# FFN activations turned in 32x32 blocks on VectorE and placed through DRAM, in a two-layer decoder trunk on one core

## The chip, the cores and the metric

The kernel runs on one core of a Trainium2 chip. The metric is the device time of one execution in microseconds. The core's engines are named as the profile names them: PE is TensorE (matmuls; PEld its weight load), DVE is VectorE, ACT is ScalarE, POOL is GpSimd, and SP is SyncE, whose queue issues the transfers.

## The reference

The reference computes a trunk of two layers on 256 tokens of width 1024, in float32. Each layer is

```python
x = x + 0.5 * swiglu(rms_norm(x, ffn1_norm[layer]), w_gate, w_up, w_down)
x = x + mixer(rms_norm(x, mix_norm[layer]), rms_norm(mem, mem_norm[layer]))
x = x + 0.5 * swiglu(rms_norm(x, ffn2_norm[layer]), w_gate, w_up, w_down)

def swiglu(h, w_gate, w_up, w_down):
    return (jax.nn.silu(h @ w_gate) * (h @ w_up)) @ w_down
```

with an inner FFN width of 2816. The mixer of layer 0 is a chunkwise mLSTM beside a cross-attention to 256 memory tokens; the mixer of layer 1 is a dilated sliding-window attention, with shared keys and values computed from layer 0's output, beside the same kind of cross-attention. The four FFNs are where the change lies.

## The kernel before

**Tiles.** The tokens lie in two tiles of 128 (`t` = 0 and 1). Each FFN's inner width is cut into `NB` = 11 blocks of `FB` = 256 columns. For block `b` and token tile `t`, `gu(b, t)` makes the gate and up products together: a PSUM bank (gups) of 128 tokens by 512 columns, 256 of gate and 256 of up, over eight chunks of the model width. `dn(b, t)` adds the down products of that block to two accumulators (acc) of 512 columns that stay in PSUM for the whole FFN.

**Precision.** Every float32 product is made from three matmuls. Each operand is split into `hi`, its value rounded to fp32r, and `lo`, the remainder (`split`, line 558: a copy on ScalarE, a subtraction on VectorE); `mm3` (line 551) multiplies hi by lo, hi by hi and lo by hi. So gu(b, t) has 24 matmuls and dn(b, t) has 12.

**Between the two products.** `hidden(b, t)` (line 761) makes the activation h: silu on ScalarE, then a multiplication on VectorE, 128 tokens by 256 columns. The down product needs h with its columns on the partitions, so TensorE transposes two squares of 128x128 into a PSUM tile (tph), and `split` copies them from there into hh and hl, the stationary operands of the down product.

**Weights.** All weights stand in one DRAM array in the order of use, as written by `_stream` (line 44) and `_pack` (line 108). A unit is 128 x 1024 values, 512 KB: a gate/up block takes four, a down block two. `load_unit` transfers a unit into one of `RAW` = 6 raw tiles on SyncE's queue, `emit_unit` casts and subtracts it into one of `RING` = 8 ring slots (hi and lo). A ring slot is free again when both token tiles have used it.

**Order.** Nothing is scheduled by a compiler: the instructions are written in the order in which the program calls them, and each engine runs its own in that order. TensorE's order is given by the loops of `ffn` (line 757). What else has to be done is held in chains of steps (`spawn`, `step`), and a planner (`_Model`, line 152 on) with its own estimates of costs decides after each group of matmuls which chain's next step is written next. Its times decide the order only; waits between engines are by semaphores. `wait` lets a chain wait for others, `finish` writes a chain to its end, `freed_bank` writes until a bank is read. The order of the products in an FFN before the change is gu(0), gu(1), dn(0), gu(2), dn(1), and so on to gu(8), dn(7), gu(9); then gu(10, 0), dn(8, 0), gu(10, 1), dn(9, 0), dn(10, 0), and dn(8, 1) to dn(10, 1). The first two blocks of the first FFN are special: `opening` (line 706) and `both` (line 741) run them for both token tiles at once, into accumulator banks, while the first transfers arrive. Two blocks, `MEMORY`, have the memory tokens' key and value product behind them.

**A path through DRAM** exists already: `shared_kv` writes a small tile (diag) to DRAM and reads it back in another layout (bias).

Of the kernel before, what the change touches and what calls it, by code (L numbers as in the profile page):

```python
# [8 lines left out]
F32 = mybir.dt.float32  # L9
F32R = mybir.dt.float32r  # L10
BF16 = mybir.dt.bfloat16
AF = mybir.ActivationFunctionType
ALU = mybir.AluOpType
# [4 lines left out]
P = 128  # L18
# [15 lines left out]
LATER = 1.5  # L34
EARLY = 0.0
WARM = 9
MEMORY = {(0, 1, 4): 0, (1, 1, 4): 1}
TAIL = 3

# [4 lines left out]
def _stream():  # L44

    units = []

    def proj(key, name, index, cols, each):
        k = 0
        while k < NK:  # L50
            n = min(each, NK - k)
            width = n * sum(b - a for _, a, b in cols)
            units.append((key + (k,), (name, index, cols, k, n), width))
            k += n

    def rows(key, name, index, order):
        for c in order:
            units.append((key + (c,), (name, index, None, c, 1), D))

    def single(key, name, index, lo, hi, kper):  # L60
        proj(key, None, index, ((name, lo, hi),), kper)

    def memory(layer):
        for m in range(2):
            units.append((("memT", layer, m), ("memT", None, None, m, 1), D))
        single(("mkv", layer), "w_mem_kv", layer, 0, 512, 2)

    def ffn(layer, which):
        g, u, d = (f"ffn{which}_w_{s}" for s in ("gate", "up", "down"))

        def gu(b):
            lo, hi = b * FB, (b + 1) * FB
            proj(("gu", layer, which, b), None, layer, ((g, lo, hi), (u, lo, hi)), 2)

        def dn(b):
            for c in range(2):
                units.append((("dn", layer, which, b, c), (d, layer, None, 2 * b + c, 1), D))

        gu(0)
        for b in range(1, NB - 1):  # L80
            gu(b)
            if (layer, which, b) in MEMORY:
                memory(MEMORY[layer, which, b])
            if b < NB - 2:
                dn(b - 1)
        gu(NB - 1)
        for b in range(NB - 3, NB):
            dn(b)

    ffn(0, 1)  # L90
    single(("a", "gq"), "a_gq", None, 0, 264, 3)
    for key, lo in (("q0", 0), ("k0", MW), ("v0", 2 * MW),
                    ("q1", 384), ("k1", MW + 384), ("v1", 2 * MW + 384),
                    ("o0", 3 * MW), ("o1", 3 * MW + 384)):
        single(("a", key), "a_w_in", 0, lo, lo + 384, 2)
    rows(("ao",), "a_w_out", 0, A_ORDER)
    ffn(0, 2)
    for b in range(3):
        single(("kv", b), "w_kv", None, b * 512, (b + 1) * 512, 2)
    ffn(1, 1)  # L100
    for b in range(2):
        single(("bq", b), "b_w_q", 0, b * 512, (b + 1) * 512, 2)
    rows(("bo",), "b_w_out", 0, B_ORDER)
    ffn(1, 2)
    return units


def _pack(units, w):

    parts = []  # L110
    for _, src, _ in units:
        name, index, cols, k, n = src
        if cols is None:
            a = w[name][index] if index is not None else w[name]
            parts.append(a[k * P:(k + 1) * P, :].reshape(-1))
            continue
        pieces = []
        for cname, lo, hi in cols:
            a = w[cname][index] if index is not None else w[cname]
            pieces.append(a[k * P:(k + n) * P, lo:hi].reshape(n, P, hi - lo))  # L120
        parts.append(np.concatenate(pieces, axis=2).transpose(1, 0, 2).reshape(-1))
    return np.concatenate(parts)
# [135 lines left out]
class _Engine:  # L258
# [5 lines left out]
    def __getattr__(self, method):  # L264
        call, model, name = getattr(self.engine, method), self.model, self.name

        def traced(out, *args, **kw):
            call(out, *args, **kw)  # L268
            aps = [a for a in list(args) + list(kw.values()) if isinstance(a, bass.AP)]
            outs = [out] + [kw[k] for k in ("accum_out",) if k in kw]  # L270
            ins = [a for a in aps if a is not kw.get("accum_out")]
            n = out.free_size()
            if name == "sync":
                model.run(name, max(n * out.partition_size() * 4 / 360e3, 0.06), outs, ins, 2.0)
                return
            fixed, each = model.COST[name]
            cost = fixed + each * n
            if method == "tensor_reduce":
                cost = fixed + each * ins[0].free_size()
            if name == "vector" and any(a.free_size() == 1 for a in ins):  # L280
                cost += 0.06
            if method == "reciprocal":
                cost = fixed + 8 * each * n
            if kw.get("accum_out") is not None or isinstance(kw.get("scale"), bass.AP):
                cost += 0.09
            if name == "gpsimd" and ALU.pow in args:
                cost = 0.4 + 0.07 * n
            for a in args if method == "activation" else ():
                table = model.TABLES.get(a) if isinstance(a, AF) else None
                if table is not None and table != model.table:  # L290
                    model.table = table
                    cost += 1.3
            model.run(name, cost, outs, ins)
        return traced
# [30 lines left out]
class _Kernel:  # L325
# [429 lines left out]


    def ffn(self, layer, which, after, memory=None):
        nc = self.nc
        acc, chains, hT = [], {}, {}

        def hidden(b, t):
            def steps(ps):
                yield from self.wait(self.stats[t])
                rstd = self.rstd[t]
                sil = self.work.tile([P, FB], F32, tag="ta", bufs=4, name="sil")
                nc.scalar.activation(sil, ps[:, :FB], AF.Silu, scale=rstd)
                yield
                h = self.work.tile([P, FB], F32, tag="ta", bufs=4, name="h")
                nc.vector.scalar_tensor_tensor(h, ps[:, FB:], rstd, sil, ALU.mult, ALU.mult)
                yield FREE  # L770
                tp = yield from self.psum("tp", [P, 512], "tph")
                for c in range(2):
                    self.transpose(tp[:, c * P:(c + 1) * P], h[:, c * P:(c + 1) * P], self.ident)
                yield
                hh = self.work.tile([P, FB], F32R, tag="hh", bufs=5, name="hh")
                hl = self.work.tile([P, FB], F32R, tag="hl", bufs=5, name="hl")
                yield from self.split(hh, hl, tp[:, :FB])
                self.leave("tp")
                hT[b, t] = (hh, hl)
            return steps  # L780

        def gu(b, t):
            chains[b, t] = self.block(t, ("gu", layer, which, b), 512, 2, hidden(b, t))

        def dn(b, t):
            if len(acc) == t:
                if t == 0:
                    self.finish(chains[0, 0], chains[0, 1])
                else:
                    self.freed_bank(*[chains[1, i] for i in range(2)])  # L790
                acc.append([self.acc.tile([P, 512], F32, tag="acc", name=f"acc{t}{h}")
                            for h in range(2)])
            self.finish(chains.pop((b, t)))
            hh, hl = hT.pop((b, t))
            last = b == NB - 1
            pairs = [(c, h) for h in range(2) for c in range(2)] if last else \
                    [(c, h) for c in range(2) for h in range(2)]
            for n, (c, h) in enumerate(pairs):
                wh, wl = self.get("dn", layer, which, b, c)
                self.until(max(self.model.ready(a) for a in (wl, hl)))  # L800
                s = slice(c * P, (c + 1) * P)
                f = slice(h * 512, (h + 1) * 512)
                self.mm3(acc[t][h], (hh[:, s], hl[:, s]), (wh[:, f], wl[:, f]),
                         b == 0 and c == 0, last and c == 1)
                if last and n % 2:
                    nc.vector.scalar_tensor_tensor(self.x[t][:, f], acc[t][h], 0.5, self.x[t][:, f],
# [6 lines left out]
        for b in range(NB - 1):  # L813
            if (layer, which, b) == (0, 1, 0):
                ps = [self.acc.tile([P, 512], F32, tag="acc", name="gups") for _ in range(2)]
                self.opening(ps, ("gu", 0, 1, 0))
                for t in range(2):
                    chains[0, t] = self.spawn(hidden(0, t)(ps[t]))
                continue
            if (layer, which, b) == (0, 1, 1):  # L820
                ps = [self.acc.tile([P, 512], F32, tag="acc", name="gups") for _ in range(2)]
                self.both(ps, ("gu", 0, 1, 1))
                for t in range(2):
                    chains[1, t] = self.spawn(hidden(1, t)(ps[t]))
            else:
                for t in range(2):
                    gu(b, t)
            if (layer, which, b) in MEMORY:
                memory()
            if 0 < b < NB - 2:  # L830
                for t in range(2):
                    dn(b - 1, t)
        gu(NB - 1, 0)
        dn(NB - 3, 0)
        gu(NB - 1, 1)
# [692 lines left out]
```

## Time and profile before

| | us |
|---|---|
| three runs | 1021.74, 1021.84, 1021.99 |
| median | 1021.84 |
| the profiled execution | 1021.66 |
| its span, first to last instruction | 1019.9 |
| TensorE busy | 1011.5 |
| TensorE weight loads | 833.3 |
| VectorE busy | 616.8 |
| ScalarE busy | 551.0 |
| GpSimd busy | 56.5 |

The profile is of one execution. Lines such as L268 and L541 are helpers: nearly every instruction has the line of the helper that writes it, so groups are read by their tiles: gups and acc are the FFN's products, tph the transposed activation, raw, hi and lo the weights. Matmuls overlap their neighbours, so a matmul's own duration is longer than the distance between two starts. Idle time of an engine that doesn't set the end costs nothing.

### The profile page before, as it was taken

How to read it: one execution, taken by the hardware profiler on the slowest of the kernel's cores; microseconds unless marked ns; L12 is line 12 of the kernel's file. 1: busy time of each engine (PE TensorE's matmuls, PEld its weight loads, DVE VectorE, ACT ScalarE, POOL GpSimd, SP SyncE). 2: the span in 40 equal slices, each digit the busy share in tenths (PEclk: the TensorE clock that was granted, in tenths of full speed). 3: DMA queues.
4: the chain of work that ended last, by engine and by line, in shares of the span. 5: the costliest groups of instructions: out<-in, count | busy, mean ns of one | idle time of the engine just before them, and what ended most of it. 6: DMA issues, size and time to landing. Idle time of an engine off the chain costs nothing.

```text
span 1019.9 us, 13096 instructions
## 1 busy us (share of the span) xinstructions
PE 1011.5 (99%) x4849; PEld 833.3 (82%) x4849; DVE 616.8 (60%) x884; ACT 551.0 (54%) x883; POOL 56.5 (6%) x82
## 2 busy tenths in 40 slices
PE   9999999999999999999999999999999999999998
PEld 6887888898988888888878888888887788888886
DVE  5855655566976746454586654745467875545452
ACT  7645545478675645454466543645457674545441
POOL 0021000010010000000021020100012000000000
PEclk9999999999999999999999999999999999999999
DMA  9854764345455565656466555656452345656531
GB/s 353 297 184 164 272 210 166 109 155 167 139 161 191 183 208 170 202 178 194 165 206 229 174 165 200 243 170 204 144 189 63 104 168 204 199 172 202 170 124 42
DMA packets 54329, 184.63 MB, mean 181 GB/s; under 512 B 6332, under 2 KB 8052, under 8 KB 54264
## 3 DMA queue, kind: packets, MB, share of 16 engines
q1 hardware_dynamic: 54120, 183.75, 53.9%
q8 instruction: 38, 0.62, 0.3%
q14 instruction: 27, 0.22, 0.1%
q10 hardware_dynamic: 144, 0.04, 0.0%
HBM read 182.70 MB, written 1.07 MB: 180 GB/s over the span
## 4 chain that ended last, share of the span: by engine, by line
PE 87%; DVE 2%; ACT 1%; issue 1%; POOL 0%; DVEq 0%; ACTq 0%
PE gups L541 42%; PE acc L541 21%; PE aps L541 7%; PE oacc L541 4%; PE kvps L541 3%; PE bqps L541 2%; PE tph L548 2%; PE tps L548 1%; PE mkvps L541 1%; PE sc L541 1%; DVE s L268 1%; DVE lo L268 1%; PE ms L541 1%; PE po L541 1%; PE pn L541 0%
## 5 line engine op out<-in xcount | busy, mean ns | idle before, releaser
L268 DVE TENSOR_TENSOR lo<-raw,hi 128x1024 fp32r<-128x1024 f32 (+3 forms) x351 | 411.8, 1192 | 151.8 <-ACT hi L268 139.0
L268 ACT CAST hi<-raw 128x1024 fp32r<-128x1024 f32 (+3 forms) x351 | 352.9, 1020 | 103.9 <-PE acc L541 58.7
L541 PE MATMUL gups<-lo,xh 128*128 128x512 f32 x704 | 278.4, 397 | 0.2 <-DVE lo L268 0.2
L541 PE MATMUL gups<-hi,xh 128*128 128x512 f32 x704 | 273.6, 390 | 0.4 <-ACT hi L268 0.4
L541 PE MATMUL gups<-hi,xl 128*128 128x512 f32 x704 | 273.7, 391 | 0.0
L541 PEld LDWEIGHTS gups<-hi,xl 128*128 128x128 f32 x704 | 132.1, 188 | 28.5
L541 PEld LDWEIGHTS gups<-hi,xh 128*128 128x128 f32 x704 | 132.5, 188 | 27.7 <-ACT hi L268 1.7
L541 PEld LDWEIGHTS gups<-lo,xh 128*128 128x128 f32 x704 | 132.2, 188 | 26.9 <-DVE lo L268 0.8
L541 PE MATMUL acc<-lo,hh 128*128 128x512 f32 x352 | 140.9, 400 | 0.0
L541 PE MATMUL acc<-hi,hl 128*128 128x512 f32 x352 | 137.6, 391 | 0.0
L541 PE MATMUL acc<-hi,hh 128*128 128x512 f32 x352 | 137.2, 390 | 0.0
L268 ACT ACTIVATE sil<-gups,rstd 128x256 f32<-128x256 f32 x88 | 41.7, 475 | 172.0 <-PE gups L541 171.9
L268 DVE SCALAR_TENSOR_TENSOR h<-gups,rstd,sil 128x256 f32<-128x256 f32 x88 | 42.2, 481 | 130.0 <-ACT sil L268 130.0
L541 PEld LDWEIGHTS acc<-hi,hl 128*128 128x128 f32 x352 | 66.0, 188 | 14.1
L541 PEld LDWEIGHTS acc<-hi,hh 128*128 128x128 f32 x352 | 66.3, 188 | 12.5
L541 PEld LDWEIGHTS acc<-lo,hh 128*128 128x128 f32 x352 | 66.1, 188 | 12.3
L268 ACT CAST hh<-tph 128x256 fp32r<-128x256 f32 x88 | 32.6, 372 | 79.1 <-PE tph L548 79.1
L268 DVE TENSOR_TENSOR hl<-tph,hh 128x256 fp32r<-128x256 f32 x88 | 37.2, 424 | 39.7 <-ACT hh L268 39.6
L541 PE MATMUL aps<-lo,xh 128*128 128x384 f32 (+1 forms) x144 | 49.5, 344 | 0.0
L541 PE MATMUL aps<-hi,xl 128*128 128x384 f32 (+1 forms) x144 | 47.5, 330 | 0.0
L541 PE MATMUL aps<-hi,xh 128*128 128x384 f32 (+1 forms) x144 | 47.4, 329 | 0.0
L268 ACT ACTIVATE xh<-tps,gains 128x128 fp32r<-128x128 f32 x96 | 27.2, 372 | 21.2 <-PE tps L548 21.2
(179 smaller groups left out, 918.6 us busy)
## 6 DMA issues: line engine op xcount, KB each, us to landing
raw<-in_wts SPq DMA_DIRECT2D x311, 512.0 KB, 4.6
raw<-in_wts SPq DMA_DIRECT2D x32, 384.0 KB, 3.5
bias<-diag SPq DMA_DIRECT2D x1, 1536.0 KB
xraw<-in_xT SPq DMA_DIRECT2D x4, 256.0 KB, 5.9
x<-in_x SPq DMA_DIRECT2D x2, 512.0 KB, 9.0
mt<-in_mem SPq DMA_DIRECT2D x2, 512.0 KB
out<-x SPq DMA_DIRECT2D x4, 256.0 KB, 2.0
raw<-in_wts SPq DMA_DIRECT2D x2, 396.0 KB, 3.5
```

The costliest lines, as they stand in the source:

```text
L268: call(out, *args, **kw)
L541: self.pe.matmul(out, lhsT=lhsT, rhs=rhs, start=start, stop=stop)
L548: self.pe.transpose(out, in_, ident)
```

## The change

A function `turned` names the blocks that are handled anew: all but the last of each FFN, and in the first FFN not blocks 0 and 1. That makes 38 of 44. For these, the activation isn't transposed on TensorE. VectorE turns each 32x32 square of h within itself (`nc.vector.transpose`), for both token tiles into one tile hb of 128 x 512. A new chain `placed` then writes hb to DRAM (256 KB) and reads it back so that the squares come to lie on the right partitions (ht, runs of 128 values, 512 bytes), both on SyncE's queue, and splits ht in one cast and one subtraction of 128 x 512 for both token tiles. The activation's columns end in another order within their 256 than before; `_pack` puts the rows of the down weights into the same order. The tiles hb, ht, hh and hl come from a pool of their own in each FFN.

The order of the products becomes gu(0), gu(1), gu(2), dn(0), gu(3), dn(1), and so on to gu(9), dn(7), and then ends as before. The stream of weights follows that order.

The planner gets a price for transfers on queues other than SyncE's; the program has one such transfer, at its start.

```diff
+def turned(layer, which, b):
+    return b < NB - 1 and ((layer, which) != (0, 1) or b > 1)
...
             if (layer, which, b) in MEMORY:
                 memory(MEMORY[layer, which, b])
-            if b < NB - 2:
-                dn(b - 1)
+            if b > 1:
+                dn(b - 2)
...
+            a = a[k * P:(k + 1) * P, :]
+            if cols:
+                a = a.reshape(4, 32, -1).transpose(1, 0, 2)
+            parts.append(a.reshape(-1))
...
+            if method == "dma_start" and name != "sync":
+                model.run(name, 1.0 if name == "gpsimd" else 0.1, outs, ins, 2.5)
+                return
...
+        def hidden_blocks(b, t):
+            def steps(ps):
+                h = self.work.tile([P, FB], F32, tag="ta", bufs=4, name="h")
+                yield from activated(ps, t, h)
+                if b not in blocks:
+                    blocks[b] = fp.tile([P, 4, 2, 2, 32], F32, tag="hb", bufs=1, name="hb")
+                nc.vector.transpose(blocks[b][:, :, :, t, :].rearrange("p j c t -> p c j t"),
+                                    h.rearrange("p (c j e) -> p c j e", c=2, j=4))
+            return steps
+
+        def placed(b, before):
+            yield from self.wait(*before)
+            hb = blocks.pop(b)
+            d = self.dram.tile([P, 512], F32, tag="hd", bufs=4, name="hd")
+            nc.sync.dma_start(d, hb.rearrange("p j c t e -> p (j c t e)"))
+            yield
+            ht = fp.tile([P, 4, P], F32, tag="ht", bufs=1, name="ht")
+            nc.sync.dma_start(ht, bass.AP(d.tensor, d.offset, [[P, P], [32 * 512, 4], [1, P]]))
+            yield
+            hh = fp.tile([P, 4, 4, 32], F32R, tag="hh", bufs=4, name="hhb")
+            hl = fp.tile([P, 4, 4, 32], F32R, tag="hl", bufs=4, name="hlb")
+            yield from self.split(*(a.rearrange("p c i e -> p i c e") for a in (hh, hl)),
+                                  ht.rearrange("p i (c e) -> p i c e", c=4))
+            for t in range(2):
+                hT[b, t] = [tuple(a[:, 2 * c + t].rearrange("p i e -> p (i e)") for a in (hh, hl))
+                            for c in range(2)]
+
+        def follow(b, t, chain):
+            made[b, t] = chains[b, t] = chain
+            if turned(layer, which, b) and t == 1:
+                chains[b, 0] = chains[b, 1] = self.spawn(placed(b, [made[b, 0], made[b, 1]]))
...
         def dn(b, t):
             if len(acc) == t:
-                if t == 0:
-                    self.finish(chains[0, 0], chains[0, 1])
-                else:
-                    self.freed_bank(*[chains[1, i] for i in range(2)])
+                self.freed_bank(*[made[t, i] for i in range(2)])
...
-            if 0 < b < NB - 2:
+            if 1 < b < NB - 1:
                 for t in range(2):
-                    dn(b - 1, t)
+                    dn(b - 2, t)
```

More of the change, by code (lines that the diff above doesn't have):

```diff
@@ L76, in dn @@
             for c in range(2):
-                units.append((("dn", layer, which, b, c), (d, layer, None, 2 * b + c, 1), D))
+                rows = "turned" if turned(layer, which, b) else None
+                units.append((("dn", layer, which, b, c), (d, layer, rows, 2 * b + c, 1), D))
         gu(0)
@@ L112, in _pack @@
         name, index, cols, k, n = src
-        if cols is None:
+        if cols is None or cols == "turned":
             a = w[name][index] if index is not None else w[name]
-            parts.append(a[k * P:(k + 1) * P, :].reshape(-1))
+            a = a[k * P:(k + 1) * P, :]
+            if cols:
+                a = a.reshape(4, 32, -1).transpose(1, 0, 2)
+            parts.append(a.reshape(-1))
             continue
@@ L757, in ffn, with ffn_in, activated @@
     def ffn(self, layer, which, after, memory=None):
+        with ExitStack() as ctx:
+            self.ffn_in(layer, which, after, memory, self.pool(ctx, f"ffn{layer}{which}"))
+    def ffn_in(self, layer, which, after, memory, fp):
         nc = self.nc
-        acc, chains, hT = [], {}, {}
+        acc, chains, hT, blocks, made = [], {}, {}, {}, {}
+        def activated(ps, t, out):
+            yield from self.wait(self.stats[t])
+            rstd = self.rstd[t]
+            sil = self.work.tile([P, FB], F32, tag="ta", bufs=4, name="sil")
+            nc.scalar.activation(sil, ps[:, :FB], AF.Silu, scale=rstd)
+            yield
+            nc.vector.scalar_tensor_tensor(out, ps[:, FB:], rstd, sil, ALU.mult, ALU.mult)
+            yield FREE
         def hidden(b, t):
             def steps(ps):
[L763 to L767, printed above, removed]
                 h = self.work.tile([P, FB], F32, tag="ta", bufs=4, name="h")
-                nc.vector.scalar_tensor_tensor(h, ps[:, FB:], rstd, sil, ALU.mult, ALU.mult)
-                yield FREE
+                yield from activated(ps, t, h)
                 tp = yield from self.psum("tp", [P, 512], "tph")
@@ L778, in steps @@
                 self.leave("tp")
-                hT[b, t] = (hh, hl)
+                hT[b, t] = [tuple(a[:, c * P:(c + 1) * P] for a in (hh, hl)) for c in range(2)]
             return steps
+        def hidden_blocks(b, t):
+            def steps(ps):
+                h = self.work.tile([P, FB], F32, tag="ta", bufs=4, name="h")
+                yield from activated(ps, t, h)
+                if b not in blocks:
[3 more added lines that the diff above has]
+            return steps
@@ new lines, in placed @@
+        def placed(b, before):
[6 more added lines that the diff above has]
+            nc.sync.dma_start(ht, bass.AP(d.tensor, d.offset, [[P, P], [32 * 512, 4], [1, P]]))
+            yield
+            hh = fp.tile([P, 4, 4, 32], F32R, tag="hh", bufs=4, name="hhb")
[5 more added lines that the diff above has]
+                            for c in range(2)]
@@ L782, in gu, with steps @@
+        def follow(b, t, chain):
+            made[b, t] = chains[b, t] = chain
+            if turned(layer, which, b) and t == 1:
+                chains[b, 0] = chains[b, 1] = self.spawn(placed(b, [made[b, 0], made[b, 1]]))
+        def steps(b):
+            return hidden_blocks if turned(layer, which, b) else hidden
         def gu(b, t):
-            chains[b, t] = self.block(t, ("gu", layer, which, b), 512, 2, hidden(b, t))
+            follow(b, t, self.block(t, ("gu", layer, which, b), 512, 2, steps(b)(b, t)))
@@ L793, in dn @@
             self.finish(chains.pop((b, t)))
-            hh, hl = hT.pop((b, t))
+            parts = hT.pop((b, t))
             last = b == NB - 1
@@ L799, in dn @@
                 wh, wl = self.get("dn", layer, which, b, c)
-                self.until(max(self.model.ready(a) for a in (wl, hl)))
-                s = slice(c * P, (c + 1) * P)
+                self.until(max(self.model.ready(a) for a in (wl, parts[c][1])))
                 f = slice(h * 512, (h + 1) * 512)
-                self.mm3(acc[t][h], (hh[:, s], hl[:, s]), (wh[:, f], wl[:, f]),
+                self.mm3(acc[t][h], parts[c], (wh[:, f], wl[:, f]),
                          b == 0 and c == 0, last and c == 1)
@@ L817, in ffn @@
                 for t in range(2):
-                    chains[0, t] = self.spawn(hidden(0, t)(ps[t]))
+                    follow(0, t, self.spawn(hidden(0, t)(ps[t])))
                 continue
@@ L823, in ffn @@
                 for t in range(2):
-                    chains[1, t] = self.spawn(hidden(1, t)(ps[t]))
+                    follow(1, t, self.spawn(hidden(1, t)(ps[t])))
             else:
```

## The prediction

> **What bounds the kernel now.** The page comes first: busy times, transfer rate by slices, the weight queue, the chain that ended last.
>
> ```profile
> span 1019.9 us, 13096 instructions
> ...
> PE 1011.5 (99%) x4849; PEld 833.3 (82%) x4849; DVE 616.8 (60%) x884; ACT 551.0 (54%) x883; POOL 56.5 (6%) x82
> ...
> GB/s 353 297 184 164 272 210 166 109 155 167 139 161 191 183 208 170 202 178 194 165 206 229 174 165 200 243 170 204 144 189 63 104 168 204 199 172 202 170 124 42
> ...
> q1 hardware_dynamic: 54120, 183.75, 53.9%
> ...
> PE 87%; DVE 2%; ACT 1%; issue 1%; POOL 0%; DVEq 0%; ACTq 0%
> ```
>
> TensorE is busy for 1011.5 of 1019.9 us and makes 87% of the chain by name. A busy share alone does not prove the bound, since matmuls overlap; the waits decide. The columns are total us, times, longest us.
>
> ```profile
> ACT hi L268 <- PE acc L541: 58.7, 59, 1.7
> ...
> ACT hi L268 <- DMA raw<-in_wts: 3.9, 4, 2.1
> ```
> ```profile
> PE warm L1418 <- DVE warm L268: 1.2, 1, 1.2
> ...
> PE gups L541 <- ACT hi L268: 0.4, 2, 0.2
> ```
> ```profile
> SPq L268 <- DVE lo L268: 753.4, 311, 13.9
> ...
> SPq L268 <- DMA diag<-rr: 2.6, 1, 2.6
> ```
>
> TensorE's longest wait in its list is 1.2 us, before the first matmul; for converted weights in the FFN it waits 0.4 us. The other way round, ScalarE's weight cast waits 58.7 us for TensorE to give a ring slot back, and only 3.9 us for a transfer. SyncE stands 753.4 us before weight loads whose raw slot is not yet free. So the feed is full from DRAM to the ring, and TensorE sets the pace. One steady stretch by engine (columns: PE, PEld, DVE, ACT, POOL busy, clock, DMA share, GB/s):
>
> ```profile
> 330.00:520.00 190.00, 190.00 (x868) 156.23 (x867) 108.08 (x133) 95.51 (x139) 2.05 (x5) 1.00 0.55 181
> ```
>
> Here VectorE is busy 57%, ScalarE 50%, the DMA engines 55%, at clock 1.00. Last, one FFN block and a half of the chain (start, us, instructions):
>
> ```profile
> 359.48 6.80 PE gups L541 x30
> 366.28 0.22 PE tph L548 x2
> 366.50 4.13 PE gups L541 x18
> 370.63 2.04 PE acc L541 x9
> 372.68 0.22 PE tph L548 x2
> 372.89 3.43 PE acc L541 x15
> 376.32 6.80 PE gups L541 x30
> 383.13 0.22 PE tph L548 x2
> 383.35 4.13 PE gups L541 x18
> ```
>
> The pattern repeats from 366.50 to 383.35: 16.85 us per block, with 48 gate/up and 24 down matmuls and two pairs of transposes (tph).
>
> **The change part by part.** *Removed: transposes on TensorE.* 38 of the 44 blocks are turned (10 in each of three FFNs, 8 in the first): 76 pairs, 152 transposes, 152 PSUM evacuations. Three readings give the price of a pair. The chain gives 0.22 us each: 76 x 0.22 = 16.7. The block period gives more: 30 gate/up matmuls take 6.80, so 0.2267 each, and 72 take 16.32; 16.85 - 16.32 = 0.53 is left for two pairs, 0.26 each: 76 x 0.26 = 19.8. The starts around one pair give the third:
>
> ```profile
> 502.72 0.48 ACT L268 ACTIVATE sil<-gups,rstd 128x256 f32<-128x256 f32 x1 [0.30 <-PE gups L541]
> ...
> 503.59 0.48 DVE L268 SCALAR_TENSOR_TENSOR h<-gups,rstd,sil 128x256 f32<-128x256 f32 x1
> ...
> 504.10 0.39 PE L541 MATMUL acc<-hi,hh 128*128 128x512 f32 x1
> ...
> 504.33 0.39 PE L541 MATMUL acc<-hi,hl 128*128 128x512 f32 x1
> ...
> 504.56 0.38 PE L548 MATMUL tph<-consts,h 128*128 128x128 f32 x2
> ...
> 504.70 0.48 PE L541 MATMUL acc<-lo,hh 128*128 128x512 f32 x1
> ...
> 505.01 0.39 PE L541 MATMUL acc<-hi,hh 128*128 128x512 f32 x1
> ```
>
> Matmuls start 0.23 apart. After the one at 504.33, the second next would have started at 504.79 and starts at 505.01: 0.22, and the following starts are a little slack. I take 0.24, the middle of 0.22 and 0.26: 76 x 0.24 = 18.2 us, ends 16.7 and 19.8. The instruction's own duration is no price, as the tph row below shows:
>
> ```profile
> L268 DVE TENSOR_TENSOR lo<-raw,hi 128x1024 fp32r<-128x1024 f32 x308 | 374.2, 1233 | 135.8 <-ACT hi L268 123.0
> L268 ACT CAST hi<-raw 128x1024 fp32r<-128x1024 f32 x308 | 320.4, 1052 | 100.2 <-PE acc L541 57.5 <-PE gups L541 24.2 <-PE oacc L541 8.0
> ...
> L268 DVE TENSOR_TENSOR hl<-tph,hh 128x256 fp32r<-128x256 f32 x88 | 37.2, 424 | 39.7 <-ACT hh L268 39.6
> L548 PE MATMUL tph<-consts,h 128*128 128x128 f32 x176 | 33.1, 271 | 0.0
> L268 ACT CAST hh<-tph 128x256 fp32r<-128x256 f32 x88 | 32.6, 372 | 79.1 <-PE tph L548 79.1
> ...
> L268 DVE TENSOR_TENSOR lo<-raw,hi 128x512 fp32r<-128x512 f32 x8 | 5.5, 692 | 5.5 <-ACT hi L268 5.5
> ...
> L268 ACT CAST hi<-raw 128x512 fp32r<-128x512 f32 x8 | 4.9, 607 | 0.6 <-DMA raw<-in_wts 0.6
> ```
>
> 271 ns times 152 would be 41 us, but the transposes overlap their neighbours. The Trainium skill, page "VectorE: DVE Perf Modes", section "The three transpose paths", lists 390 ns for a TensorE transpose of 128x128 bf16; by that the sum would be 59 us and the kernel near 962. The trace, with 0.22 a pair, speaks against using either duration.
>
> *Added on VectorE.* Two block turns of 128x256 per turned block. No such row exists; the nearest is hl, 128x256, 424 ns. One 128x512 subtraction (nearest row lo 128x512, 692) replaces two of 424. So VectorE per block goes from 6 x 1.233 + 2 x 0.481 (the h instruction, 0.48 above) + 2 x 0.424 = 9.21 to 9.21 - 0.85 + 0.69 + 0.85 = 9.90 us. ScalarE gets lighter: 0.607 for 2 x 0.372. Both lie under 16.3 us of TensorE; cost taken: 0. VectorE has 16.3 - 9.05 = 7.3 us for the two turns, so this cover is gone only where one takes over 3.6 us. Lower end below nothing: excluded, since TensorE doesn't wait for these engines.
>
> *Added DMAs.* Per turned block a 256 KB write to DRAM and a 256 KB read back, both on SyncE's in-order queue among the weight loads: 38 x 0.52 = 20 MB more on 184. Rows of landing times:
>
> ```profile
> raw<-in_wts SPq DMA_DIRECT2D x311, 512.0 KB, 4.6
> ...
> xraw<-in_xT SPq DMA_DIRECT2D x4, 256.0 KB, 5.9
> x<-in_x SPq DMA_DIRECT2D x2, 512.0 KB, 9.0
> ...
> out<-x SPq DMA_DIRECT2D x4, 256.0 KB, 2.0
> ```
>
> The write is like out<-x, same size: 2.0 us. The read is bounded by 2.0 and by 9.0 (the start, where DMA was crowded); I take 4.6, the steady weight load's. Before the write, SyncE waits for the second token tile's turn; before the read, for the write's landing. Behind it wait weight loads, then ScalarE's casts. The write's 2.0 us (2.6 for diag, above) per 16.3 us is idle queue time of the kind SyncE already spends 753 us in; the loads held up then go out together. Cover: six raw slots and eight ring slots, each worth 12 matmuls, 2.7 us. Cost 0; the far end is a rival.
>
> *New waits.* ScalarE's cast of the placed tile waits for the read, and behind it in its queue stand weight casts and the next silu. If the planner is 3 us too early each time, ScalarE loses 3 of about 8 spare us per block, and the PSUM bank whose silu is late is next needed two products (10.9 us) later: 0.
>
> *Moved: down products one block later.* Same matmuls, same 4 + 2 weight units per block; the two weight loads on SyncE, their casts and subtractions go behind the four of the next gate/up block in each queue, in the order in which TensorE now uses them, so the lead of eight ring slots stays. The placed tile of block b has dn(b-2), gu(b+1), dn(b-1), gu(b+2) as cover: 144 x 0.2267 = 32.6 us. For block 9 it is shorter: dn(7), gu(10,0), dn(8,0), gu(10,1), 84 matmuls, 19.0 us. The path needs 0.30 until silu, 1.35 to the end of h, 0.42, 2.0, 4.6, 0.61, 0.69: 10.0 us. 9 us are to spare. At the start of each FFN, dn(0) gets more cover; TensorE did not wait there, so 0. The un-turned last block keeps its old path. Space: the new tiles share memory with the mixers' pools; those wait for dn(9,1), with dn(10,1), 2.7 us, behind it: 0.
>
> Sum: 1021.66 (profiled run: span 1019.9 and 1.8 around it) - 18.2 = 1003.5. The median of the runs shown, 1021.84, stands 0.18 above it, so I say 1003.6.
>
> **The rivals.** (1) *Block 9 comes late.* With 5.9 for the write and 9.0 for the read and one long cast and subtraction ahead in each queue (1.05 + 1.23) the path is 20.6 us, 1.6 over its 19.0; four FFNs lose 6.4: 1010. Against: those rows come from the crowded first microseconds, while the write out<-x takes 2.0.
>
> (2) *Slower: SyncE's order starves the ring.* The six loads, 3.1 MB, at the peak slice's 353 GB/s take 8.9 us and the new 0.52 MB 1.5: 10.4 of 16.3 us. If the queue moves nothing while SyncE waits, 5.9 us per block are free for waiting; from 6.4 us the whole gain is eaten (38 x 0.48 = 18.2). At 7.0 us: 38 x 1.1 - 18.2, so 1045. For it: each block has two dependent waits in one queue. Against: one write's landing is 2.0 to 2.6 us, and transfers in flight go on meanwhile.
>
> (3) *It does not do what it says: TensorE is not full.* Weight loads into TensorE cover 82%; were the pace set by the feed, removing transposes would leave gaps: 1021.7. The Trainium skill, "Perfetto Trace Analysis", section "Identifying the Most-Contended Engine", says matmul busy share is a bad measure and to judge headroom by the load share. The trace disagrees here as far as the waits go: it is ScalarE that waits for TensorE.
>
> (4) *VectorE becomes the bound*, if a turn takes over 3.6 us, 8.6 times its nearest row. At 4.2 us each block grows by 2 x 0.55 over 16.3: 38 x 1.1 - 18.2, again 1045. The Trainium skill, "VectorE: DVE Perf Modes", section "Rules for kernel authors", advises TensorE for 128x128 where PSUM will do; by that rule this change should not pay. No row here shows a turn on VectorE.
>
> **How the numbers follow.** Forecast 0.78; rival (1) 0.08; (2) 0.07; (3) 0.04; (4) 0.03. Faster 0.86, same 0.04, slower 0.10; same means within 0.2%, 2 us, about what this kernel's measurement can tell. The forecast's own range: 16.7 to 19.8 gives 1002 to 1005; the planner orders everything else anew, for which I allow its total waits at TensorE, about 3 us, either way: 999 to 1008. To leave out no more than 2 in 10 the range takes in rival (1): 999 to 1012.
>
> **What would show it.** Right: 24 tph left of 176; pieces of 24 or more matmuls unbroken at 0.227; a block period of 16.3 to 16.4; TensorE's waits still under a few us; VectorE busy up by about 26 us (38 x 0.69), ScalarE down by 5. The write lands in 2 to 3 us, the read in about 5. Wrong: gaps in TensorE before the last down products (rival 1), casts that wait for weight transfers far over 3.9 us (2), matmul starts spaced wider than 0.227 with no tph (3), turns near 4 us (4).

## The result, and the profile after

| | before | after |
|---|---|---|
| median of the runs, us | 1021.79 | 1008.36 (1006.85 to 1009.91) |
| ratio, 95% interval | | 0.9869 (0.9848 to 0.9891) |
| the profiled execution, us | 1021.66 | 1009.91 |

The change is 13.4 us faster, 1.3%. The profiled execution of after is the longest of its four, which matters below. One execution among the experiments, at a granted clock of 0.85, took 1102 us and is left out of the numbers of its kernel ("Turned, in the old order"). The page of after:

```profile
span 1008.2 us, 13017 instructions
...
PE 996.4 (99%) x4697; PEld 820.4 (81%) x4697; DVE 630.8 (63%) x922; ACT 544.5 (54%) x845; POOL 56.7 (6%) x82
...
PE 85%; DVE 3%; ACT 1%; DMA 1%; POOL 1%; issue 1%; DVEq 0%; ACTq 0%; SPq 0%
...
L278 DVE STREAM_TRANSPOSE hb<-h 128x256 f32<-128x256 f32 x76 | 33.6, 442 | 19.6 <-DMA hd<-hb 18.6
L278 ACT CAST hhb<-ht 128x512 fp32r<-128x512 f32 x38 | 23.6, 622 | 33.2 <-DMA ht<-hd 33.0
...
hd<-hb SPq DMA_DIRECT2D x38, 256.0 KB, 5.7
ht<-hd SPq DMA_DIRECT2D x38, 256.0 KB, 3.8
```

TensorE is still the bound, 996.4 of 1008.2 us busy. tph is gone from the named part of the chain by line, and hd<-hb, the write to DRAM, stands in it with 1%. TensorE's idle time is 1008.2 - 996.4 = 11.8 us, against 8.4 before.

Where the 11.7 us of span came from is read off the chain. Each FFN starts with a piece of 9 gate/up matmuls and ends with a piece of 33 (in the last FFN 54) down matmuls. First before, then after (start, us, instructions):

```profile
197.74 7.51 PE acc L541 x33
...
330.73 2.09 PE gups L541 x9
...
509.94 7.51 PE acc L541 x33
...
554.77 2.08 PE gups L541 x9
...
745.77 7.51 PE acc L541 x33
...
829.97 2.09 PE gups L541 x9
...
1003.52 12.30 PE acc L541 x54
```
```profile
196.19 7.52 PE acc L554 x33
...
329.19 2.09 PE gups L554 x9
...
504.76 7.65 PE acc L554 x33
...
549.70 2.08 PE gups L554 x9
...
739.59 7.65 PE acc L554 x33
...
823.92 2.08 PE gups L554 x9
...
992.23 12.31 PE acc L554 x54
```

| stretch | before | after | difference | blocks turned |
|---|---|---|---|---|
| FFN one, to 197.74 + 7.51 and 196.19 + 7.52 | 205.25 | 203.71 | -1.54 | 8 |
| mixer A | 125.48 | 125.48 | 0.00 | |
| FFN two | 186.72 | 183.22 | -3.50 | 10 |
| shared keys and values | 37.32 | 37.29 | -0.03 | |
| FFN three | 198.51 | 197.54 | -0.97 | 10 |
| mixer B | 76.69 | 76.68 | -0.01 | |
| FFN four | 185.85 | 180.62 | -5.23 | 10 |
| to the end | 4.08 | 3.66 | -0.42 | |

The mixers did not move. FFN four has 5.23 us for 10 blocks, 0.52 a block and 0.26 a pair: the upper of the prediction's readings. At this rate 38 blocks are worth 19.9 us; 11.2 of them appear in the four FFNs. FFN two lacks 1.7, FFN one 2.6, FFN three 4.3: 8.6 us in all. Two places account for about 7.3 of them; 1.3 I cannot place. These are figures of one execution: FFN one, which is the same in three of the experiments below, took 203.71 us here and 202.82, 202.37 and 202.84 there. The first place is the pace of the down products; a block in FFN two, then in FFN four:

```profile
378.86 5.60 PE acc L554 x24
384.45 10.91 PE gups L554 x48
...
873.42 5.44 PE acc L554 x24
878.86 10.88 PE gups L554 x48
```

24 down matmuls take 5.60 us in FFN two (and three) and 5.44 in FFN four (and one), with no wait between them. Eight pieces of 0.16, 0.03 in each gate/up piece between them and 0.13 in the last piece (7.65 against 7.52 in FFN one) add up to about the 1.7. The second place is the stretch of the memory products, in FFN one and three (columns as in the prediction's table by stretch; then TensorE's waits):

```profile
60.00:100.00 40.00, 37.69 (x166) 30.36 (x165) 22.54 (x29) 20.86 (x34) 5.09 (x8) 1.00 0.67 217
...
600.00:645.00 45.00, 43.07 (x188) 34.20 (x187) 26.52 (x34) 22.48 (x30) 7.14 (x4) 1.00 0.63 204
```
```profile
PE mkvps L554 <- DVE h L278: 1.6, 2, 1.4
PE gups L554 <- DVE lo L278: 1.5, 3, 0.5
...
PE tpk L561 <- DVE kn L278: 1.2, 1, 1.2
```

TensorE idles 2.31 us in the first and 1.93 in the second stretch; before, it idled 0.27 and 0.08 there, so 3.9 us are new. It waits for the gate/up bank that h must free (mkvps), for weights (lo) and for the normed memory keys (kn). The other two waits that the change made:

```profile
ACT hhb L278 <- DMA ht<-hd: 33.0, 30, 2.8
...
DVE hb L278 <- DMA hd<-hb: 18.6, 6, 4.3
```

### The profile page after: what moved, and what is told of

The parts are those of the page before. It is cut to its first block, busy times and chain, and to the rows that moved or that the text cites. A ratio compares the mean times of both kernels' runs of the same rounds, so it can differ in the third digit from the quotient of the medians.

```text
span 1008.2 us, 13017 instructions
## 1 busy us (share of the span) xinstructions
PE 996.4 (99%) x4697; PEld 820.4 (81%) x4697; DVE 630.8 (63%) x922; ACT 544.5 (54%) x845; POOL 56.7 (6%) x82
## 4 chain that ended last, share of the span: by engine, by line
PE 85%; DVE 3%; ACT 1%; DMA 1%; POOL 1%; issue 1%; DVEq 0%; ACTq 0%; SPq 0%
PE gups L554 41%; PE acc L554 22%; PE aps L554 7%; PE oacc L554 4%; PE kvps L554 3%; PE bqps L554 2%; PE tps L561 1%; DVE lo L278 1%; PE sc L554 1%; DVE s L278 1%; DMA hd<-hb 1%; PE ms L554 1%; PE po L554 1%; POOL rp_e L278 1%; PE pn L554 0%
## 5 line engine op out<-in xcount | busy, mean ns | idle before, releaser
L278 DVE TENSOR_TENSOR lo<-raw,hi 128x1024 fp32r<-128x1024 f32 (+3 forms) x351 | 407.4, 1182 | 129.1 <-ACT hi L278 124.5
L554 PE MATMUL gups<-lo,xh 128*128 128x512 f32 x704 | 274.3, 391 | 1.5 <-DVE lo L278 1.5
L554 PE MATMUL acc<-lo,hhb 128*128 128x512 f32 x304 | 120.5, 396 | 0.0
L554 PE MATMUL acc<-hi,hlb 128*128 128x512 f32 x304 | 119.3, 393 | 0.0
L554 PE MATMUL acc<-hi,hhb 128*128 128x512 f32 x304 | 119.3, 392 | 0.0
L554 PEld LDWEIGHTS acc<-hi,hlb 128*128 128x128 f32 x304 | 57.1, 188 | 12.9
L554 PEld LDWEIGHTS acc<-hi,hhb 128*128 128x128 f32 x304 | 57.2, 188 | 12.2
L554 PEld LDWEIGHTS acc<-lo,hhb 128*128 128x128 f32 x304 | 57.1, 188 | 12.1
L278 DVE STREAM_TRANSPOSE hb<-h 128x256 f32<-128x256 f32 x76 | 33.6, 442 | 19.6 <-DMA hd<-hb 18.6
L278 ACT CAST hhb<-ht 128x512 fp32r<-128x512 f32 x38 | 23.6, 622 | 33.2 <-DMA ht<-hd 33.0
```

The source lines that it names most:

```text
L554: self.pe.matmul(out, lhsT=lhsT, rhs=rhs, start=start, stop=stop)
```

## The experiments

Theory at the start: the removed pairs are worth what FFN four shows, and two unplanned costs take 8.6 us back, one set by where the new tiles lie in SBUF, one by the placement's work among the memory products. Rivals: the order costs it, or SyncE's queue.

### Price of a pair, alone

```diff
-                for c in range(2):
-                    self.transpose(tp[:, c * P:(c + 1) * P], ...)
+                for _ in range(2):
+                    for c in range(2):
+                        self.transpose(tp[:, c * P:(c + 1) * P], ...)
```

> The kernel before, with each pair of activation transposes written twice into the same PSUM columns (88 more pairs). It prices the removed term by itself, without any of the placement. By the block period (0.26 us a pair) 22.9 us are added, 1044.5; by the chain's pieces (0.22) 19.4, 1041. Rival (a transpose is hidden between matmuls, so the gain came from elsewhere): under 5 us, below 1027.

Measured 1041.36 against 1021.63, ratio 1.0194 (1.0164 to 1.0223): 19.7 us for 88 pairs, 0.224 each. The chain of this kernel shows the doubled pair at 0.44:

```profile
365.82 6.80 PE gups L541 x30
372.63 0.44 PE tph L548 x4
373.07 4.13 PE gups L541 x18
```

So a pair that is added behind another costs the chain's 0.22. Taking a lone pair out gives 0.26: the 18 gate/up matmuls behind a pair take 4.13 us, where 18 x 0.2267 would be 4.08, and this slack is there once, whether one pair or two stand ahead. The transposes were not hidden.

### The order alone

```diff
 def turned(layer, which, b):
-    return b < NB - 1 and ((layer, which) != (0, 1) or b > 1)
+    return False
...
-hh = self.work.tile([P, FB], F32R, tag="hh", bufs=5, name="hh")
+hh = self.work.tile([P, FB], F32R, tag="hh", bufs=6, name="hh")
```

> Only the order of the change: down products two blocks behind, no block turned, TensorE transposes all 44 (hh and hl have 6 buffers instead of 5, for the longer wait). Theory (the order costs nothing; the new stalls beside the memory products come from the placement): 1021.8 within 1 us, TensorE idle about 8.4 us as before. Rival (the order itself makes the stalls at the memory products, since the down block's weights come later): 4 us slower, 1026, with gaps in TensorE right after the memory products of both layers.

Measured 1022.20 against 1021.58, ratio 1.0009 (0.9999 to 1.0018): no change that can be told. The order by itself makes no stall.

### Turned, in the old order

```diff
-            if 1 < b < NB - 1:
+            if 0 < b < NB - 2:
                 for t in range(2):
-                    dn(b - 2, t)
+                    dn(b - 1, t)
```

(and the same in the weight stream)

> The changed kernel with the order of before: down products one block behind. Theory (the path from the end of a gate/up block to its hlb takes 16.6 us in the changed kernel's trace, so it needs the second block of cover): with dn(b-1) and gu(b+1), 16.3 us, as cover each of some 34 blocks waits about 0.3 us, and the last turned block of each FFN, with 13.6 us of cover, 3 us: 10 + 12, so about 1030. Rival (transfers come earlier when the order leaves more room): within 2 us of 1008.

Measured 1017.86, the median of seven executions from 1015.02 to 1021.06, ratio 0.9966 (0.9948 to 0.9984): 9.5 us slower than the change with its own order, less than half of what the theory said. It missed the place, too: in the steady part of FFN two no block waits. TensorE waits for the first placed tile of FFN two, three and four, some 1.5 us each, at the memory products, and 0.3 to 0.5 us for h at the ends of three FFNs. Two rows of its list:

```profile
PE acc L554 <- ACT hhb L278: 2.6, 2, 1.3
...
PE tph L561 <- DVE h L278: 1.2, 3, 0.5
```

The second block of cover is needed, but not because each block is 0.3 us late.

### Where the tiles lie

The stationary operands hhb and hlb and the moving one, the weight ring, start at fixed bytes of each partition. Modulo 256, hhb and hlb start where the ring does in FFN one and four, and 64 past it in FFN two and three. Moving everything by 32 bytes:

```diff
+        self.const.tile([P, 8], F32, name="pad")
         self.mhalf = self.const.tile([P, 16], F32, name="mhalf")
```

> The changed kernel with a pad of 32 bytes per partition ahead of everything in SBUF. All operands that TensorE reads start 32 bytes past a multiple of 64 in both kernels: the x tiles and weight ring at 224 past a multiple of 256, hhb and hlb at 224 in the first and last FFN (24 down matmuls in 5.44 us) and at 32 in the two middle ones (5.60 us). With the pad the former stand at 0 and the latter at 64. Theory (the start address modulo 64, 128 or 256 sets the distance of matmuls): the middle FFNs' 24 down matmuls fall to 5.44 or less, and if 0 is better than 224 all 512-wide matmuls come closer than 0.2267 us, down to 0.2133 at best; at 0.220 some 3700 of them give 25 us, so below 985. Rival (where in SBUF the tile lies, above some 208 thousand bytes, sets it): nothing moves, 5.44 and 5.60 stay, 1008.

Measured 1008.14, ratio 0.9869 (0.9855 to 0.9884), with 5.60 in the middle FFNs and 5.44 in the others as in the change: nothing moved. A shift of all operands together does nothing. Next, pads of different size in the pools of the FFNs:

```diff
+        pad = {(0, 2): 48, (1, 2): 16}.get((layer, which))
+        if pad:
+            fp.tile([P, pad], F32, name="pad")
```

> The changed kernel with a pad in the FFN pool: 192 bytes in the second FFN (hhb and hlb then start 224 past a multiple of 256, as in the first), 64 bytes in the last (32 past, as the second had it), none in the first and third. Theory (address modulo 64 to 256): 24 down matmuls take 5.44 us in FFN one, 5.44 in two, 5.60 in three, 5.60 in four. Rival (height in SBUF): 5.44, 5.60, 5.60, 5.44 as in the changed kernel. Total 1008 either way, since one gain and one loss of 1.6 us cancel.

1008.65 in one run. A block of FFN two and one of FFN four:

```profile
393.65 5.44 PE acc L554 x24
...
886.99 5.60 PE acc L554 x24
```

They changed places, as the theory has it, and FFN two became 1.74 us shorter (327.85 to 509.33, 181.48). Height in SBUF is out. Since a common shift does nothing and a relative one does, the distance between the two operands is the next theory. Two more kernels measured other distances, by the same edit with other pads:

> The changed kernel with a pad of its own in each FFN's pool, so that hhb and hlb start 32, 128, 192 and 96 bytes (FFN one to four) past where the weight ring starts, modulo 256. Known so far: 0 gives 5.44 us for 24 down matmuls, 64 gives 5.60, and moving both together changes nothing. Theory (the distance between the two operands' starts modulo 256 sets it): other values at some of the four, and the same within an FFN. First rival (only the multiple of 256 counts): 5.60 at all four. Second rival (a distance exists at which the two reads never meet): under 5.44 at one of them, 5.12 at best (512 columns in 0.2133 us).

> The changed kernel with pads such that hhb and hlb start 160, 224, 64 and 224 bytes past the weight ring modulo 256 (FFN one to four). Measured so far for 24 down matmuls: 0: 5.44, 32: 5.59, 64: 5.60, 96: 5.61, 128: 5.59, 192: 5.49. Theory (the distance modulo 256 alone sets it): the two FFNs at 224 agree though they lie 30 thousand bytes apart, and 64 gives 5.60 again; 160 lies between 5.49 and 5.59. Whether 224 goes below 5.44 is open: if the cost falls steadily from 128 on over 192 to 256, 224 is between 5.44 and 5.49. Rival (something else of each FFN's pool matters too): the two at 224 differ by 0.05 or more.

They took 1010.59 and 1012.22 in one run each. Two rows of either, for distances 32, 192, 160 and 224:

```profile
137.11 5.59 PE acc L554 x24
...
662.68 5.49 PE acc L554 x24
```
```profile
136.76 5.60 PE acc L554 x24
...
379.54 5.59 PE acc L554 x24
```

| distance modulo 256 | 0 | 32 | 64 | 96 | 128 | 160 | 192 | 224 |
|---|---|---|---|---|---|---|---|---|
| 24 down matmuls, us | 5.44 | 5.59 | 5.60 | 5.61 | 5.59 | 5.60 | 5.49 | 5.59 |

The two FFNs at 224 agree, and 64 gives 5.60 again. The start of hhb and hlb by itself is out: in FFN one they start at a multiple of 256 both with the common shift, where the ring does too (5.44), and at distance 32, where the ring starts at 224 (5.59). So the distance sets it. The pads move hb and ht along with hhb and hlb; that the latter count is concluded from which matmuls are slow. The guesses about the curve fell: 160 and 224 are slow, only 0 is best, 192 is near it, and none is below 5.44. Then the pad where it helps:

```diff
+        if (layer, which) in ((0, 2), (1, 1)):
+            fp.tile([P, 48], F32, name="pad")
```

> The changed kernel with a pad of 192 bytes in the FFN pools of the second and third FFN, so that hhb and hlb start 0 past the weight ring modulo 256 in all four. Theory (the uneven start costs the two middle FFNs 1.74 us each, as the second FFN's stretch in the padded kernel showed): 1008.4 - 3.5 = 1004.9, 24 down matmuls in 5.44 us everywhere. Rival (what is saved in the down products is lost to waits, as the feed has no more room): the 5.44 are there, the time stays at 1007 or above.

Measured 1004.12, ratio 0.9829 (0.9814 to 0.9843): 4.2 us less than the change, 3.5 expected, with 5.44 in all FFNs. FFN two (328.32 to 509.80, 181.48) is now 5.24 us shorter than before the change, as FFN four is. FFN three became 3.16 us shorter than in the change's profiled execution, of which 1.3 is less idle time among the memory products and does not belong to the pads. This cause is shown.

### The memory products

```diff
+    near = which == 1 and b in (3, 4)
-    return b < NB - 1 and ((layer, which) != (0, 1) or b > 1)
+    return b < NB - 1 and not near and ((layer, which) != (0, 1) or b > 1)
```

> The changed kernel, but blocks 3 and 4 of the two FFNs with memory products are not turned (34 turned instead of 38). Theory (the placement of these two blocks falls into the memory products and costs about 2 us of TensorE's time in each): 4 blocks of 0.53 us are given back, 2.1, and 3.4 us of idle time go; TensorE idle about 8.4 us, the time 1007. Rival (the stalls do not come from the placement): idle time stays near 11.8 and the time is 1010.5.

Measured 1006.56, ratio 0.9855 (0.9839 to 0.9872), 1.8 us less than the change with four blocks fewer turned; the two intervals overlap, so the time alone does not tell. The profile does. Its page has TensorE's idle time at 1004.4 - 996.4 = 8.0 us, and the first of the two stretches is back at 0.27 us idle:

```profile
span 1004.4 us, 13026 instructions
...
PE 996.4 (99%) x4713; PEld 821.7 (82%) x4713; DVE 630.0 (63%) x918; ACT 544.3 (54%) x849; POOL 54.6 (5%) x82
```
```profile
60.00:100.00 40.00, 39.73 (x178) 32.01 (x177) 21.23 (x27) 21.47 (x35) 5.09 (x8) 1.00 0.59 203
```

The second, 600 to 645, idles 0.08 us. Both are the figures of before the change, so the gaps belong to the turning and placement of these two blocks. With the pads as well:

> The same pads, and blocks 3 and 4 of the two FFNs with memory products not turned. Theory (the two losses are separate and add): 1006.6 of the kernel without these four turned, less 1.7 in the second FFN and 1.3 in the seven slow blocks of the third: 1003.5, TensorE idle about 8. Rival (they overlap): 1005 or more.

1003.73, ratio 0.9826 (0.9811 to 0.9841), near the 1003.5 of losses that add; from the pads alone, 1004.12, it can't be told apart. Is it ScalarE's standing before ht, or the added work itself?

```diff
             nc.sync.dma_start(ht, bass.AP(d.tensor, d.offset, [[P, P], [32 * 512, 4], [1, P]]))
-            yield
+            yield 3.0 if b < NB - 2 else 0.0
```

> The same pads, all 38 blocks turned, and the planner places the cast of ht 3 us later (not for block 9). Theory (the gaps beside the memory products come from ScalarE standing before ht, which holds up silu and the casts behind it): ScalarE's wait for ht falls from 33 us to under 5, the gaps from 3.4 us to about 1, 1004.9 - 2.4 = 1002.5. Rival (the gaps come from the placement's cast and subtraction themselves falling into the crowded stretch): ScalarE's wait falls, the gaps stay, 1004.9 or more.

```profile
ACT hhb L278 <- DMA ht<-hd: 7.8, 7, 1.8
```
```profile
60.00:100.00 40.00, 39.32 (x176) 32.24 (x175) 23.77 (x30) 23.30 (x35) 5.97 (x8) 1.00 0.70 235
...
600.00:645.00 45.00, 43.43 (x193) 35.41 (x192) 28.09 (x34) 22.25 (x29) 7.74 (x4) 1.00 0.67 221
```

ScalarE's wait fell from 28.1 us with the pads alone to 7.8. The two stretches idle 0.68 + 1.57 = 2.25 us, with the pads alone 1.62 + 0.61 = 2.23. The sums speak for the rival. But 0.9 us of the second stretch is a wait for the memory keys' norm, which a GpSimd instruction held up in this execution and not in that of the pads alone (more of it below). Without it 1.35 would be left, near the theory's 1. The time, above the theory's 1002.5 and below the rival's 1004.9, does not settle it either. So this run leaves open whether the wait for ht makes part of the gaps. The time, 1003.30, ratio 0.9822 (0.9806 to 0.9839), is the lowest measured, 0.8 below the pads alone, which lies inside both intervals. These three padded kernels all beat before and the change; which of them is best is open.

### The queue of the write

```diff
-            nc.sync.dma_start(d, hb.rearrange("p j c t e -> p (j c t e)"))
+            nc.scalar.dma_start(d, hb.rearrange("p j c t e -> p (j c t e)"))
```

> The changed kernel with the write of hb on ScalarE's queue instead of SyncE's; the read stays on SyncE's. Theory (the write lands after 5.7 us, not 2.0, because it stands behind weight loads in SyncE's ring): it lands in 2 to 3 us, ScalarE's 33 us of waiting for ht nearly vanish, the gaps beside the memory products shrink from 3.4 us to 1 or less, 1005.5. Rival (the DMA engines are busy, whatever the queue): it still lands after 5 us or more and the time stays at 1008.

Measured 1015.89, ratio 0.9943 (0.9919 to 0.9966): 7.5 us slower than the change. The write from ScalarE's queue and the waits:

```profile
hd<-hb ACTq DMA_DIRECT2D x38, 256.0 KB, 5.7
```
```profile
ACT hhb L278 <- DMA ht<-hd: 127.0, 38, 11.4
...
ACT hi L278 <- DVE hb L278: 43.9, 17, 2.7
```

It still lands after 5.7 us, so the theory fell: the place in SyncE's queue is not what makes it long. That the time would rise neither theory nor rival had. ScalarE, which casts the weights, now stands before VectorE's turn (43.9 us) and longer before ht (127.0). What is special about a short one is seen in the changed kernel's last write, which the read follows as soon as it has landed:

```profile
969.63 2.46 SPq L278 DMA_DIRECT2D raw<-in_wts  x2
974.79 0.33 SPq L278 DMA_DIRECT2D hd<-hb  x1
976.80 0.38 SPq L278 DMA_DIRECT2D ht<-hd  x1
```

No weight load is issued after 972.09, and this write takes 2.0 us. The rest, 5.7 in the median, have loads in flight beside them. That the engines' load sets it fits both; no run varied it by itself.

## Why the prediction was right, and where it was not

The forecast was 1003.6, the measured median 1008.36, inside the range and 4.8 us above. It lies 0.4 us outside 999 to 1008, which the forecast's own mechanism was given; the rest of the range was room for rival (1), which did not happen. And a gain 1.7 us larger than forecast covered part of 8.6 us that the sum had at nothing. So that the number held is in part luck; the mechanism, removed transposes against TensorE's bound, is not.

- *TensorE is the bound, and removing pairs gives their time back*: right, shown by the doubled pairs and by FFN four. The term 76 x 0.24 = 18.2 was 1.7 too small; the block period's 0.26 was the right reading, since it holds the disturbed neighbours too. Neither 271 ns of the row nor the 390 ns of the Trainium skill's page "VectorE: DVE Perf Modes", section "The three transpose paths", could have given it.
- *VectorE*: the turn takes 442 ns against 424 of its nearest row, the cast and subtraction of 128 x 512 take 622 and 688. The cover held; rival (4) is out. VectorE's busy time rose by 14.0 us, not 26. The rows added and removed come to 27.5, lo is 4.5 shorter, and all of VectorE's rows together rise from 635.5 to 658.3, by 22.8; the other 8.8 are time in which neighbouring instructions overlap, which the page counts once (616.8 and 630.8).
- *Cost 0 for the down products*: this step failed. "Same matmuls" took for granted the same pace. The list of signs had the right symptom, starts wider than 0.227 with no tph, but put it down to rival (3). Two FFNs lost 1.7 us each to the place of a pool, which no row of before could show, as hh lay at distance 0 in all FFNs.
- *New waits: 0*: this failed as well, but only beside the memory products. The argument was made for a steady block. In the stretches of the memory products ScalarE has waits of its own already before (in the second 7.1 us for mkvps), and TensorE's one wait for weights between 60 and 760, 0.2 us, stands in the first. With the turn and placement of two blocks there, 3.9 us more of TensorE's time are gone. That they cause it is shown by the kernel without them; by which wait is not: in FFN three 1.2 us of the 1.93 are the wait for the memory keys' norm below.
- *The write's 2.0 us*: the row was from the kernel's end, where no loads run; in the stream it is 5.7. The path is 16.6 us from the end of gate/up to hlb (873.42 to 890.04 in FFN four), not 10.0. The cover of 32.6 bears it. Block 9, with 19.0, bears it too: no gap stands before its down products, and rival (1) did not happen.
- *SyncE's order starves the ring*: did not happen in steady blocks, although SyncE now waits 81.7 us for these writes.
- *The order, 0*: right, 1.0009.

One more part of the profiled execution depends on the moment. The GpSimd instruction for the memory keys' norm, 128 x 4 values, in the change, in the kernel with even pads, and in the one with the later cast:

```profile
634.48 4.03 POOL L278 TENSOR_SCALAR rp_e<-hss 128x4 f32<-128x4 f32 x1
```
```profile
631.13 0.29 POOL L278 TENSOR_SCALAR rp_e<-hss 128x4 f32<-128x4 f32 x1
```
```profile
627.41 4.63 POOL L278 TENSOR_SCALAR rp_e<-hss 128x4 f32<-128x4 f32 x1
```

It runs beside four weight subtractions on VectorE. In the first they last from 633.49 to 638.11; it starts 0.99 us behind their start, ends 0.4 us behind their end, and TensorE waits 1.16 us for its result. In the second it starts 0.98 us behind their start and is done after 0.29; with the first pads it starts 0.98 us behind as well and takes 4.03, so what decides is finer than the trace shows. Of the eleven kernels with turned blocks, five have the long one in their trace and six a short one. With 1.93 us idle in that stretch against 0.61, it accounts for at most 1.3 of the 3.1 us between the changed kernel's shortest and longest run. Only one execution of each kernel has a trace, so whether the shorter ones were spared it is not shown.

## What to carry to other kernels

When new tiles become operands of the bounding engine, compare the pace of its instructions, stretch by stretch, with that of before: a slower pace without any wait is a cost that no list of waits shows, and a pad may mend it. Work that is hidden in the steady part must also be carried through the places where that cover is thin; look for them in the profile first, and price a landing from rows with the same traffic beside it. To price an instruction that overlaps its neighbours, take the period of a repeating block with and without it, not its duration.

## What the runs showed of the hardware

- TensorE's pace hung on where its stationary operand lay against its moving one: with hhb and hlb at distance 0 from the weight ring modulo 256 bytes, 512-wide matmuls came every 0.2267 us, at other distances as late as 0.234 (5.61 for 24). Why is not shown. The Trainium skill, page "SBUF — State Buffer", section "SBUF: two separate sides", says that TensorE's ports wait on no other engine; these rows don't contradict that: here TensorE's own two operands matter.
- A 256 KB write to DRAM took 2.0 us behind the last weight load, and in the stream 5.7 in the median, from SyncE's queue and from ScalarE's alike.
- A GpSimd instruction of 0.29 us took 4.03 beside VectorE subtractions. The Trainium skill, the same page, section "Who interferes with whom", says that a VectorE instruction with two SBUF inputs contends with GpSimd's reads; the trace agrees in that the long one ended just behind the four subtractions. In other kernels the same instruction, as far behind the first subtraction, took 0.29, so it isn't always held up.
- VectorE's turn of 128 x 256 in 32x32 squares took 0.442 us.
